# GpSimd issues its loads in program order instead of the scheduler's order, in a weight-gradient matmul with seven products for eight

## The chip, the cores and the metric

The kernel runs on one core of one Trainium2 chip. The metric is the device time of one execution in microseconds (us), as the median of several runs. The profile is one execution on the same core; its span, 166.3 us, is the part between the first and the last recorded instruction and is about 2 us shorter than the device time.

## The reference

```python
def setup_inputs():
    batch, m, k, n = 16, 512, 1024, 768
    return {
        "input": np.random.randn(batch, m, k).astype(np.float32),
        "grad_output": np.random.randn(batch, m, n).astype(np.float32),
    }

def reference(input: np.ndarray, grad_output: np.ndarray) -> np.ndarray:
    grad_weight = np.einsum('bmk,bmn->kn', input, grad_output)
    return grad_weight.astype(np.float32)
```

Batch and rows are one contraction of 16 x 512 = 8192 rows: the output, 1024 x 768, is the sum over all rows of x (1024 columns) times g (768 columns). Both inputs are float32 in the chip's main memory, 33.6 MB and 25.2 MB.

## The kernel before, in words

**Slices and loads.** The 8192 rows are 64 slices of 128 rows. `LOADS` has 32 letters, one for each load `u` of two slices. Eight loads `s` come first, then twenty `P`, then four `s`. An `s` gives two single items, one a slice. A `P` gives one item of two slices, which is computed with fewer products (below). For each load there is a tile `xp` (128 x 2 x 1024, bf16) and a tile `gp` (128 x 2 x 768, bf16). GpSimd issues the transfers that fill them, and these turn float32 into bf16 on the way. For the first eight loads (`u < MERGED`) each slice has its own transfer: `gp` on line 111 (192 KB written), `xp` on line 113 (256 KB). From load 8 on there is one transfer of both slices: `gp` on line 106 (384 KB), `xp` on line 107 (512 KB). In the program `gp` stands ahead of `xp` each time. The very first data (`xf` for slices 0 and 1, `gf` for slice 0) come as float32 through the queues of SyncE and ScalarE and are rounded by VectorE and ScalarE on line 203.

**Buffers.** `gp` and `xp` of load 0 have a pool of their own. All later ones, with `xf` and `gf`, share a pool of `PAIRS_HELD = 14` buffers for each of the two kinds, so a load may be issued when an earlier tile in its buffer is done with. Each GpSimd transfer also signals on one of eight semaphores, taken in turn. A transfer waits until the one issued eight before it has landed. So at most eight are under way at once.

**Products.** For an `s` item the output is four quadrants, called A, B (upper rows), C, D (lower rows); A and C take the left columns of g, B and D the right ones. For a `P` item the two slices and the two halves of columns form a 2 x 2 by 2 x 2 block product, done with seven products instead of eight: A and D, and five others `n p m o q`. They need sums and differences of halves: `ge` from `gp` (lines 131, 135), `gp` changed in place (line 140), `xe` from `xp` (lines 145, 149), `xp` in place (line 154). VectorE makes these, all in bf16.

**TensorE.** `ORDER` is written out by hand. A step such as `A9` means: bring product A up to item 9, with the weights from x and the moving operand from g, 128 x 384 at a time into a bank (line 278), for four blocks q. `A9!0,0,0,0` also closes the product: its four banks are added to the float32 sums `acc` or `macc`, by ScalarE (line 292) or VectorE (line 296), and after block q the given number of VectorE's sums for coming pairs (`filler`) is placed there. At the end `macc` is shared out to `acc` (line 163 and others), and finished blocks go to memory through SyncE's queue. The first steps are:

```
"A1:4 C1:4!0,0,0,0 B2:4!0,0,0,0 A2 D1:2 A3!0,0,0,0 D2 D3 D4 C4:4!0,0,0,0 D5 B5:2 D6!0,0,0,0 "
"B6 A6:2 B7 B8 A7 A8 A9!0,0,0,0 ...
```

**What sets the order on each engine.** A planner orders the instructions of an engine by its own estimate of times, unless the engine is named in `manual_schedule`. Before the change TensorE, VectorE and ScalarE are named, so they run in the order of the program. GpSimd is not, so its transfers stand in the planner's order.

Of the kernel before, what the change touches and what calls it, by code (L numbers as in the profile page):

```python
# [42 lines left out]
def kernel(  # L43
# [30 lines left out]
    SLOT = {"n": 0, "p": 1, "m": 2, "o": 3, "q": 4}  # L74

    E = mybir.EngineType
    ctx.enter_context(tc.manual_schedule(engines={E.PE, E.DVE, E.Activation}))

    xf = [pairs.tile([P, K], f32, name=f"xf{s}", tag="xp") for s in range(2)]
    gf = pairs.tile([P, N], f32, name="gf", tag="gp")  # L80
# [308 lines left out]
```

## Time and profile before

| | |
|---|---|
| device time, median of 3 runs | 168.19 us (168.03 to 168.38) |
| span of the profile | 166.3 us |
| TensorE (PE) busy | 159.8 us, 96% of the span |
| VectorE (DVE) busy | 118.6 us, 71% |
| ScalarE (ACT) busy | 87.6 us, 53% |
| GpSimd (POOL) busy | 41.1 us, 25% |
| granted TensorE clock | 1.00 |
| moved by DMA, as the page counts it | 33.39 MB, of it 28.64 MB through GpSimd's queue |

The page lists groups of instructions as: line, engine, operation, output tile and input tile, shape, count; then busy time, mean of one, and the idle time of the engine just ahead of them with what ended it. A timeline row is: start, duration, engine, line, operation, tiles, count, and in brackets the idle time before it and its releaser. GpSimd's rows in it (`DMA_DIRECT2D`) are [...]0.53 us each, not the transfer itself. A transfer's landing is the last of sixteen increments of its semaphore[...].

### The profile page before, as it was taken

Reading aid. Unit: us, or ns where it says so; the run is one execution under the profiler, and the core shown is the slowest. Engines: PE = TensorE matmul, PEld = TensorE weight load, DVE = VectorE, ACT = ScalarE, POOL = GpSimd, SP = SyncE. Lnnn points to the kernel's source line nnn. Section 1 sums busy time; section 2 is a strip of 40 time slices with the busy share of each in tenths; the row PEclk is TensorE's granted clock in tenths of the full one; section 3 lists DMA queues with packets and bytes.
Section 4 is the critical chain, followed back from the end, with each engine's and each line's share of the span. In section 5 each row is a group of like instructions: output and inputs, shape, how many; then the busy total and the mean of one; then the engine's idle time right before and its main releaser. Section 6 shows DMA issues by size and latency. Waiting matters only on the chain.

```text
span 166.3 us, 2688 instructions
## 1 busy us (share of the span) xinstructions
PE 159.8 (96%) x963; PEld 93.5 (56%) x963; DVE 118.6 (71%) x240; ACT 87.6 (53%) x206; POOL 41.1 (25%) x81
## 2 busy tenths in 40 slices
PE   8799999999999999999999999899999999999992
PEld 2356656565655655665565655455656656565661
DVE  0400221121979879878979998989999899999992
ACT  3779413330486768755648476756677878100000
POOL 7444444544122222222212222222221000000000
PEclk9999999999999999999999999999999999999999
DMA  5999999999999999999999999999999999105555
GB/s 181 287 209 208 211 206 208 208 209 217 211 216 211 215 212 214 210 215 210 215 211 214 211 213 212 217 211 212 212 217 213 214 210 209 25 0 189 189 189 189
DMA packets 14124, 33.39 MB, mean 201 GB/s; under 512 B 1568, under 2 KB 5920, under 8 KB 14112
## 3 DMA queue, kind: packets, MB, share of 16 engines
q0 software_dynamic: 11088, 28.64, 88.5%
q1 hardware_dynamic: 2736, 3.54, 6.0%
q10 hardware_dynamic: 288, 1.05, 1.7%
q8 instruction: 7, 0.11, 0.3%
q14 instruction: 5, 0.04, 0.1%
HBM read 58.72 MB, written 3.15 MB: 372 GB/s over the span
## 4 chain that ended last, share of the span: by engine, by line
PE 76%; DVE 16%; DMA 5%; POOL 1%; issue 1%; DVEq 0%; POOLq 0%
PE bank L278 75%; DVE macc L296 5%; DMA xp<-in_input_dram 5%; DVE gp L140 2%; DVE xe L145 2%; DVE acc L296 2%; DVE ge L131 2%; DVE xp L154 1%; POOL gp L111 1%; DVE ge L135 1%; DVE xe L149 1%; PE bank L328 0%; DVE acc L336 0%; DVEq L296 0%; POOLq L373 0%
## 5 line engine op out<-in xcount | busy, mean ns | idle before, releaser
L278 PEld LDWEIGHTS <-xp 128*128 128x128 bf16 x697 | 67.6, 98 | 49.4 <-issue 1.9
L278 PE MATMUL bank<-gp,xp 128*128 128x384 bf16 x537 | 92.4, 326 | 2.0 <-DVE xp L203 0.8
L292 ACT COPY acc<-bank 128x384 f32<-128x384 f32 x55 | 24.4, 487 | 31.2 <-PE bank L278 31.1
L296 DVE TENSOR_TENSOR acc<-bank,acc 128x384 f32<-128x384 f32 x46 | 23.7, 552 | 21.3 <-PE bank L278 21.0
L292 ACT COPY macc<-bank 128x384 f32<-128x384 f32 x61 | 27.3, 492 | 20.2 <-PE bank L278 20.1
L278 PEld LDWEIGHTS <-xe 128*128 128x128 bf16 x240 | 23.2, 98 | 16.6 <-DVE xe L145 1.4
L278 PE MATMUL bank<-ge,xp 128*128 128x384 bf16 x160 | 29.8, 326 | 0.2
L278 PE MATMUL bank<-gp,xe 128*128 128x384 bf16 x160 | 28.3, 326 | 0.3 <-DVE xe L145 0.2
L296 DVE TENSOR_TENSOR macc<-bank,macc 128x384 f32<-128x384 f32 x37 | 19.4, 553 | 5.3 <-PE bank L278 5.0
L107 POOL DMA_DIRECT2D xp<-in_input_dram x24 | 12.7, 530 | 36.9 <-DMA xp<-in_input_dram 20.3
L106 POOL DMA_DIRECT2D gp<-in_grad_output_dram x24 | 12.7, 530 | 32.7 <-PE bank L278 19.5
L268 ACT COPY bank<-macc 128x384 f32<-128x384 f32 x43 | 19.3, 490 | 0.0
L268 ACT COPY bank<-acc 128x384 f32<-128x384 f32 x41 | 18.4, 501 | 0.0
L163 DVE TENSOR_TENSOR acc<-acc,macc 128x768 f32<-128x768 f32 x16 | 14.5, 950 | 0.0
L145 DVE TENSOR_TENSOR xe<-xp 128x1024 bf16<-128x1024 bf16 x20 | 13.7, 684 | 0.7 <-DMA xp<-in_input_dram 0.7
L278 PE MATMUL bank<-ge,xe 128*128 128x384 bf16 x80 | 14.1, 326 | 0.0
L154 DVE TENSOR_TENSOR xp<-xp 128x1024 bf16<-128x1024 bf16 x20 | 13.7, 683 | 0.0
L131 DVE TENSOR_TENSOR ge<-gp 128x768 bf16<-128x768 bf16 x20 | 11.0, 550 | 0.1
L140 DVE TENSOR_TENSOR gp<-gp 128x768 bf16<-128x768 bf16 x20 | 11.0, 551 | 0.0
L113 POOL DMA_DIRECT2D xp<-in_input_dram x14 | 7.5, 538 | 9.0 <-DMA xp<-in_input_dram 6.4
L111 POOL DMA_DIRECT2D gp<-in_grad_output_dram x15 | 8.2, 547 | 6.1 <-DMA gp<-in_grad_output_dram 4.6
L294 DVE COPY acc<-bank 128x384 f32<-128x384 f32 x2 | 1.0, 554 | 10.6 <-PE bank L278 10.6
(19 smaller groups left out, 34.3 us busy)
## 6 DMA issues: line engine op xcount, KB each, us to landing
xp<-in_input_dram POOLq DMA_DIRECT2D x24, 512.0 KB, 16.9
gp<-in_grad_output_dram POOLq DMA_DIRECT2D x24, 384.0 KB, 16.7
xp<-in_input_dram POOLq DMA_DIRECT2D x14, 256.0 KB, 8.5
gp<-in_grad_output_dram POOLq DMA_DIRECT2D x15, 192.0 KB, 8.5
out_dram<-acc SPq DMA_DIRECT2D x15, 192.0 KB, 1.9
xf<-in_input_dram ACTq DMA_DIRECT2D x2, 512.0 KB, 5.0
gf<-in_grad_output_dram SPq DMA_DIRECT2D x2, 192.0 KB, 4.3
out_dram<-acc SPq DMA_DIRECT2D x1, 128.0 KB, 1.7
```

The lines of the kernel that those rows point to most:

```text
L106: nc.gpsimd.dma_start(out=gp, in_=G[rows, :].rearrange("(p m) n -> p m n", m=2))
L107: nc.gpsimd.dma_start(out=xp, in_=X[rows, :].rearrange("(p m) k -> p m k", m=2))
L111: nc.gpsimd.dma_start(out=gp[:, h, :], in_=G[s * P : (s + 1) * P, :])
L131: nc.vector.tensor_add(out=ge[:, 0:2, :], in0=g[:, :, 0, :], in1=g[:, :, 1, :])
L140: nc.vector.tensor_sub(out=g[:, 1:3, :], in0=g[:, 1:3, :], in1=g[:, 3::-3, :])
L145: nc.vector.tensor_add(out=xe[:, 0:2, :].rearrange("p a k -> p (a k)"), in0=xp[:, 0, :], in1=xp[:, 1, :])
L154: nc.vector.tensor_sub(out=x[:, 1:3, :], in0=x[:, 1:3, :], in1=x[:, 0::3, :])
L163: nc.vector.tensor_add(out=dst, in0=dst, in1=macc[:, slots, q, :])
L268: nc.scalar.copy(out=bank, in_=sum_of(p, q))
L278: nc.tensor.matmul(bank, stat, mov, start=opening and j == 0 and not carried, stop=close and j == len(items_now) - 1, skip_group_check=car ...
L292: nc.scalar.copy(out=dst, in_=bank)
L296: nc.vector.tensor_add(out=dst, in0=bank, in1=dst)
```

## The change

```diff
     E = mybir.EngineType
-    ctx.enter_context(tc.manual_schedule(engines={E.PE, E.DVE, E.Activation}))
+    ctx.enter_context(tc.manual_schedule(engines={E.PE, E.DVE, E.Activation, E.Pool}))
```

GpSimd (`Pool`) is named as well, so its 77 transfers are issued as the program has them: `gp` and then `xp` of each load, load by load. The aim is that data are asked for in the order in which the program uses them. The number and the sizes of the transfers, the instructions of all other engines, and the buffers' addresses remain. In two places the order of issue is a different one. Loads are numbered from 0; h0 and h1 are the two slices of a load:

```
place 1   before: gp0 h1, gp1 h0, gp1 h1, xp1 h0, xp1 h1, gp2 h0, ...
          after:  gp0 h1, gp1 h0, xp1 h0, gp1 h1, xp1 h1, gp2 h0, ...

place 2   before: ... gp23 xp23 xp24 xp25 gp24 gp25 gp26 gp27 xp26 gp28 xp27 xp28 gp29 xp29 xp30 gp30 gp31 xp31
          after:  ... gp23 xp23 gp24 xp24 gp25 xp25 gp26 xp26 gp27 xp27 gp28 xp28 gp29 xp29 gp30 xp30 gp31 xp31
```

## The prediction

> **What bounds the kernel now.** I read the head of the page first, then the chain that ended last, then the waits of TensorE's two rows, of VectorE and of GpSimd, and then the timeline of the places that the change touches.
>
> ```profile
> PE 159.8 (96%) x963; PEld 93.5 (56%) x963; DVE 118.6 (71%) x240; ACT 87.6 (53%) x206; POOL 41.1 (25%) x81
> DMA  5999999999999999999999999999999999105555
> PE 76%; DVE 16%; DMA 5%; POOL 1%; issue 1%; DVEq 0%; POOLq 0%
> ```
>
> PE is all but full, and the DMA engines are full until about 142 us. The chain is PE for three quarters; its DVE part lies between 63 and 124 us, where PE stops eight times, mostly for DVE, 2.6 us in all by the starts of its matmuls. That stretch has the same instructions after the change. What the change can touch is waiting for loads. The waits of PE's weight loads and of DVE (total us, times, longest), then the chain's first pieces:
>
> ```profile
> PEld L278 <- DMA xp<-in_input_dram: 0.8, 2, 0.6
> DVE xe L145 <- DMA xp<-in_input_dram: 0.7, 1, 0.7
> ```
>
> ```profile
> 1.23 1.70 POOL gp L111 x3
> 2.93 7.67 DMA xp<-in_input_dram
> 10.65 52.52 PE bank L278 x322
> ```
>
> In the whole run PE's weight loads waited twice for a load, and DVE's sums once. The chain says that the first of these, the landing of xp1 h0, set the start of 52 us of unbroken PE work. The timelines of PEld and PE show both:
>
> ```profile
> 10.64 12.79 PEld L278 LDWEIGHTS <-xp 128*128 128x128 bf16 x80 [0.59 <-DMA xp<-in_input_dram]
> 23.64 1.42 PEld L278 LDWEIGHTS <-xp 128*128 128x128 bf16 x10 [0.20 <-DMA xp<-in_input_dram]
> ```
>
> ```profile
> 7.61 2.83 PE L278 MATMUL bank<-gp,xp 128*128 128x384 bf16 x15 [0.56 <-DVE xp L203]
> 10.65 35.92 PE L278 MATMUL bank<-gp,xp 128*128 128x384 bf16 x220 [0.20 <-DMA xp<-in_input_dram]
> ```
>
> The second wait cost PE nothing: its weight load came late, but the matmul behind it started at 23.659, one normal step of 0.1625 us after the one ahead (23.496). It has no slack either. This is xp4 h0, which step `A9` needs. The timeline of GpSimd shows why it cannot come sooner:
>
> ```profile
> 2.93 1.08 POOL L113 DMA_DIRECT2D xp<-in_input_dram  x2
> 12.18 0.53 POOL L113 DMA_DIRECT2D xp<-in_input_dram  x1 [0.77 <-DMA xp<-in_input_dram]
> 14.35 0.53 POOL L113 DMA_DIRECT2D xp<-in_input_dram  x1 [0.73 <-DMA xp<-in_input_dram]
> 23.88 0.53 POOL L113 DMA_DIRECT2D xp<-in_input_dram  x1 [0.49 <-DMA xp<-in_input_dram]
> ```
>
> Each issue starts about 0.28 us after the landing of the transfer issued eight before it. xp4 h0 is issued at 14.35 and lands, by its last semaphore event, at 23.59; the issue eight later starts at 23.88. So eight transfers are always queued and the pace is that of the data.
>
> [...] So an order of issue moves places in one line and makes no bandwidth; the trace agrees, with landings every 0.91 to 0.95 us for 192 KB and 1.2 to 1.3 us for 256 KB. [...] The trace shows seven packets of 16 KB on the instruction queue, about 20 us apart at first (the work of 128 matmuls takes 20.8 us), the first at 20.456 us, lasting 0.945 us. It falls on a single DMA engine: of gp4 h0's sixteen increments fifteen came by 21.62, the last at 22.58, and xp4 h0's fifteenth came at 22.88, its last at 23.59. That is what makes xp4 h0 the tight one.
>
> **The change part by part.** The instructions of PE, DVE and ACT and the buffers' addresses are the same in both programs. No transfer is added or removed, so GpSimd's 77 issues cost what they did. What moves:
>
> Place 1. The third and fourth transfers in line swap. Before, by the landing events: gp1 h0 8.40, gp1 h1 9.35, xp1 h0 10.60, xp1 h1 11.90. After: xp1 h0 at 8.40 + 1.25 = 9.65, gp1 h1 at 10.60, and xp1 h1 at 11.90 as before. The matmul ahead of the wait started at 10.121, so the next can start at 10.121 + 0.1625 = 10.284 instead of 10.648: PE gains **0.36 us** here. gp1 h1 is needed at 12.61 - 0.36 = 12.25 and is there at 10.60.
>
> Then the gain meets the next loads. The need of each before less 0.36, against its landing: xp1 h1 12.09 against 11.90; xp2 h0 14.69 against 14.06; xp2 h1 17.29 against 16.31; xp3 h0 20.54 against 18.47; xp3 h1 21.19 against 20.72; xp4 h0 23.28 against **23.59**. The last fails. Its landing is unchanged, since the same bytes and the same instruction fetch lie ahead of it on the slowest engine. PE stops there and starts again where it did: weights at 23.635, matmul at about 23.64 against 23.659. Left of 0.36 us: about **0.01 to 0.02 us**.
>
> One second-order effect: PE ahead by 0.36 asks for its fetch at about 20.09 instead of 20.456. On the slow engine this is inside xp3 h1 and no longer behind it, and could delay xp3 h1 by up to 0.945, to 21.66. Its weights would then load at about 21.70, its matmul start at about 21.71, against 21.71 before. So the gain would go at xp3 h1 already; the result is the same.
>
> One wait is other: the issue of xp3 h0 waits for the third transfer, now at 9.65 instead of 9.35. It starts about 0.3 us later, at 9.93, and behind it GpSimd's next issue waits for 10.60 as before. Seven transfers are queued meanwhile, some 7.5 us of data; hidden.
>
> Place 2. xp24 and xp25 go behind their gp, xp26 and xp27 likewise. From xp23 (108.41), with 1.85 us for a gp and 2.45 for an xp as in the landings before, after: gp24 110.3, xp24 112.7, gp25 114.6, xp25 117.0, gp26 118.9, xp26 121.3, gp27 123.2, xp27 125.6, gp28 127.5, xp28 130.0, gp30 136.1, xp30 138.6. First uses before: gp24 115.59, xp24 117.62, gp25 119.62, xp25 121.75, gp26 124.22, xp26 126.59, gp27 128.13, xp27 129.57, gp28 and xp28 138.2; loads 29 to 31 from 142.9 on. The shortest slack is 3.9 us, where before gp24 had 0.38. But DVE did not wait for gp24 either: its rows are closed.
>
> ```profile
> 115.13 0.55 DVE L296 TENSOR_TENSOR macc<-bank,macc 128x384 f32<-128x384 f32 x1
> 115.59 0.55 DVE L131 TENSOR_TENSOR ge<-gp 128x768 bf16<-128x768 bf16 x1
> ```
>
> So place 2 gains nothing and costs nothing. Its waits for free buffers are on work done 20 us or more earlier (by the release times in the trace of before), and the last landing stays at about 142.9. Sum: -0.02 us, for a time of 168.19 - 0.02 = **168.17 us**.
>
> **Rivals.** (a) The head start is kept, because xp4 h0 lands sooner in the new order or in most runs. For it: PE's work is unbroken from 10.65 to 63.2, so what is gained there goes on. Against it: xp4 h0 had no slack, and the line ahead of it holds the same bytes. It gives 168.19 - 0.36 = 167.83; half of it kept, 168.0. (b) Slower: the later issue of xp3 h0 (0.3 us), or the earlier fetch, delays xp4 h0 or xp3 h1 beyond the need. For it: xp4 h0 passes each delay to PE one for one, and the fetch of 0.945 us is known to decide here. Against it: seven transfers are queued. It gives 168.19 + 0.30 = 168.49. (c) Place 2 helps, if DVE in ordinary runs is often held by gp24; the profile has slack of 0.38 there and DVE's list of waits has no such row, so at most a few tenths: about 167.9.
>
> **How the numbers follow.** Forecast (gain lost at xp4 h0, place 2 hidden) 0.72; (a) 0.12; (c) 0.05; (b) 0.11. So faster 0.17, same 0.72, slower 0.11. 0.2% is 0.34 us. The range takes in the full gain and the full loss and about 0.1 us of scatter, since three runs before lay within 0.17 us of their median: 167.73 to 168.58.
>
> **What would show it.** Right: PE's first long block starts at about 10.28, PE stops 0.2 to 0.4 us at a weight load at about 21.7 or 23.6 with an xp transfer as releaser, and from 23.7 to 124 us the rows are those of before. GpSimd's last issue stays near 125.6. Wrong: no stop there and DVE's first wait at 63.27 moved to about 62.9 (rival a), or that wait moved to 63.5 or later (rival b), or DVE rows between 115 and 130 us that move against PE's (c).

## The result, and the profile after

| | before | after |
|---|---|---|
| device time, median of 6 runs | 168.22 us (168.03 to 168.65) | 168.12 us (167.85 to 168.46) |
| ratio after/before, 95% interval | | 0.9995 (0.9978 to 1.0012) |
| span of the profile | 166.3 us | 166.7 us |

The change makes no difference that these runs can tell. A second set of 13 runs of the changed kernel (run e5 below) gave 1.0002 (0.9994 to 1.0010).

The head of the page is nearly what it was, but the DMA share is gone from the chain that ended last:

```profile
PE 160.6 (96%) x963; PEld 94.1 (56%) x963; DVE 118.5 (71%) x240; ACT 87.6 (53%) x206; POOL 41.0 (25%) x81
...
PE 80%; DVE 16%; ACT 1%; issue 1%; DVEq 0%
```

The chain in order of time (start, us, what) shows what took its place:

```profile
0.78 4.64 PE bank L89 x12
5.42 1.53 PE bank L278 x5
6.95 0.02 issue
6.97 1.63 ACT acc L292 x4
8.60 0.61 ACT xp L203 x2
9.21 0.05 issue
9.26 54.30 PE bank L278 x333
```

In this execution TensorE did not wait for xp1 h0 at all. It was late for another reason: the twelve warm-up matmuls and the first real ones ran at half speed for longer. The warm-up matmuls of 512 columns start 0.43 us apart up to 5.00 us in the profile after; in the one before they do so up to 4.14 us, and then 0.26 and 0.22 us apart. The first real matmuls start 0.32 us apart in the profile after and 0.16 us apart in the one before. The busy time of each engine in the stretch from 4.2 to 6.7 us (in brackets how many instructions started there; TensorE comes first), before and then after, has 13 matmuls against 10. The granted clock, third from the end, reads 1.00 in both and does not show it:

```profile
4.20:6.70 2.50, 2.17 (x13) 1.12 (x12) 1.20 (x5) 1.55 (x5) 1.40 (x3) 1.00 1.08 336
```

```profile
4.20:6.70 2.50, 2.50 (x10) 1.16 (x9) 1.14 (x5) 1.04 (x3) 1.39 (x3) 1.00 1.08 337
```

The trace's clock events have full speed from 4.22 us on before and from 6.72 us on after. The moment varies from run to run, and what sets it is not shown: in the thirteen of the fourteen profiles of this study that recorded it (all but e10), it lies between 3.50 and 6.75 us, and kernels with the same start have it early (e4, 3.94 us) and late (the profile after, 6.72 us). In the profile after, ScalarE's first bank copies (line 292) start at 6.97 us, where they started at 6.20 before; the rounding of slice 1 stands behind them (line 203, to 9.21 us), and xp1 h0 is long there (9.79 us) when TensorE comes to it at 10.89. In the old order it would have landed at about 10.74 (an estimate: the landing of gp1 h1, which has taken its place in the line), still in time. In such an execution place 1 has nothing to give.

Place 2 is as predicted. gp24 lands at 110.36 us and is used at 115.98; in VectorE's timeline the row (line 131) follows the one ahead of it without a gap, as before:

```profile
115.51 0.55 DVE L296 TENSOR_TENSOR macc<-bank,macc 128x384 f32<-128x384 f32 x1
115.98 0.55 DVE L131 TENSOR_TENSOR ge<-gp 128x768 bf16<-128x768 bf16 x1
```

### The profile page after: what moved, and what is told of

The parts are those of the page before. It is cut to its first block, busy times and chain, and to the rows that moved or that the text cites. A ratio compares the mean times of both kernels' runs of the same rounds, so it can differ in the third digit from the quotient of the medians.

```text
span 166.7 us, 2688 instructions
## 1 busy us (share of the span) xinstructions
PE 160.6 (96%) x963; PEld 94.1 (56%) x963; DVE 118.5 (71%) x240; ACT 87.6 (53%) x206; POOL 41.0 (25%) x81
## 4 chain that ended last, share of the span: by engine, by line
PE 80%; DVE 16%; ACT 1%; issue 1%; DVEq 0%
PE bank L278 77%; DVE macc L296 5%; PE bank L89 3%; DVE gp L140 2%; DVE xe L145 2%; DVE acc L296 2%; DVE ge L131 2%; DVE xp L154 1%; ACT acc L292 1%; DVE ge L135 1%; DVE xe L149 1%; PE bank L328 0%; DVE acc L336 0%; ACT xp L203 0%; DVEq L296 0%
## 5 line engine op out<-in xcount | busy, mean ns | idle before, releaser
L278 PE MATMUL bank<-gp,xe 128*128 128x384 bf16 x160 | 28.3, 326 | 0.3 <-DVE xe L145 0.2
```

Source lines behind the costliest of these rows:

```text
L278: nc.tensor.matmul(bank, stat, mov, start=opening and j == 0 and not carried, stop=close and j == len(items_now) - 1, skip_group_check=car ...
```

## The experiments

The theory: place 1 gives TensorE a head start, and a load that lands just in time takes it back; place 2 moves loads that are early in either order. Rivals: one place gains what the other loses; the head start is hardly ever there; what stands behind it is not a load. In the runs that move single loads the transfers are put in a list and issued in the order of the list, with some names moved behind others; all else is the changed kernel. The ratios are estimated from all runs of both kernels and differ by up to 0.0006 from the quotient of the medians. The kernel before, run beside them, has a median of 168.30 us for e1 to e4, 168.35 for e5 to e8 and 168.41 for e9 to e12.

**e1, place 1 alone, and e2, place 2 alone.**

```diff
 e1:
+    moved = {"x24": "x23", "x25": "x24", "x26": "g27", "x27": "g28", "g30": "x30"}   # late loads as before
 e2:
+    moved = {"x1.0": "g1.1"}                                                         # early loads as before
```

> Place 1 alone: xp1 h0 ahead of gp1 h1 as in the change, the late loads in the old order. Theory (the head start is lost at xp4 h0, which has no slack): within 0.1 us of before, 168.2. Theory that place 1 gains and place 2 gives it back: 0.36 us faster, 167.85. Theory that place 1 costs through a later issue: 0.3 us slower, 168.5. In a profile whose clock is granted early, PE's long block starts at about 10.28 and PE stops some 0.3 us at a weight load at 21.7 or 23.6; in one whose clock is granted late, neither is there.

> Place 2 alone: the early loads in the old order, the late ones gp, xp, gp, xp as in the change. Theory (the late loads are early enough in both orders): within 0.1 us of before, 168.2, and VectorE's rows from 108 to 130 us keep their distances. Theory that place 2 hides a loss or a gain of its own: 0.2 to 0.4 us off before, with VectorE or TensorE waiting for a load between 110 and 143 us.

Measured: e1 168.46 us, ratio 1.0011 (1.0005 to 1.0018) in 21 runs; e2 168.25 us, 0.9996 (0.9988 to 1.0004). So place 2 does nothing, and place 1 alone gains nothing and may cost a tenth of a per cent. TensorE's weight loads in e1:

```profile
9.01 12.63 PEld L278 LDWEIGHTS <-xp 128*128 128x128 bf16 x79 [0.80 <-ACT xp L203]
22.53 7.43 PEld L278 LDWEIGHTS <-xp 128*128 128x128 bf16 x47 [0.90 <-DMA xp<-in_input_dram]
```

The clock came late in this profile (6.23 us), and xp1 h0's weights were loaded at 10.65 us, no earlier than in the profile before. In the old order they would have had to wait until about 10.87 here (an estimate, again from the landing of gp1 h1), so some 0.2 us were gained. The wait at 22.53, which stops TensorE's matmuls for 0.68 us, takes more than that. It is for xp3 h1. Fifteen of its sixteen increments had come by 20.97, the last came at 22.49. TensorE's first instruction fetch (that it is TensorE's is inferred; the last section says from what), one packet of 16 KB, had started at 20.453 and took 0.949 us. The DMA queues from 20.3 to 21.5 us show it (queue, kind: packets, MB, share of the time of 16 engines):

```profile
q0 software_dynamic: 159, 0.24, 109.0%
q8 instruction: 1, 0.02, 4.9%
```

So in e1 the fetch fell into xp3 h1's packets, and one of that load's sixteen increments came 1.52 us after the other fifteen. Before, it started at 20.456 too, when xp3 h1 was not yet through either (15th increment 20.69, last 20.72), but did not hold it up. What differs is how much of the load was left. Take the time from the fetch's start to the moment when the load would have been there without it; where the load was held up, that moment is estimated as its 15th increment and the lag that xp3 h0 had behind its own. It is 0.71 us in e1 and 0.93 to 1.03 us in e4, e9 and e11, which were held up. It is 0.26 to 0.56 us in the profiles where the fetch started within xp3 h1 and did not hold it up (before, e2, e3, e6, e10).

**e3 and e4, the old and the program's order, with xp4 h0 needed later.** Product A is closed one item earlier, and C8 comes ahead of B9. By the order of the matmuls this also moves the first use of xp3 h1 four matmuls (0.65 us) later, and that of xp4 h1 and xp5 h0 four matmuls sooner:

```diff
-    "B6 A6:2 B7 B8 A7 A8 A9!0,0,0,0 B9 C9:2 C10!0,0,0,0 B11 ...
+    "B6 A6:2 B7 A7 A8!0,0,0,0 B8 C8:2 B9 C9 C10!0,0,0,0 B11 ...
```

> Old order of loads, and TensorE's hand order changed so that item 8 (xp4 h0) is needed 16 matmuls, 2.6 us, later: A closes after item 7 and C8 comes before B9. All is computed. Theory: alone it gains nothing, 168.2, because PE is not held up by xp4 h0 in the old order (0.00 to 0.02 us).

> Program order of loads as in the change, with the same later need of item 8. Theory (xp4 h0 takes the head start): with it out of the way the head start of 0.36 us goes through to VectorE's first wait and the end, up to 0.36 us below the old order with the same hand order, 167.85, in executions whose clock is granted early. Rival (the start itself is set by when the full clock is granted and by the rounding of slice 1, not by xp1 h0, in most executions): no difference to the old order in those, PE's long block starting at 9.2 to 9.3 without a wait for xp1 h0 in both, and a difference of the medians well under 0.36 us.

Measured: e3 168.21 us, 0.9992 (0.9986 to 0.9999); e4 168.22 us, 0.9990 (0.9981 to 0.9998). The two orders don't differ by more than the runs scatter. For e3 no gain was expected; its interval lies just below 1. Two other profiles of the old order show what the later need can save: TensorE stopped 0.18 us for xp4 h0 in e6 (landed at 24.00 us) and 0.06 us in e2, and in e3 it doesn't. The clock was granted early in both profiles (3.50 and 3.94 us), so they can be laid side by side. TensorE's weight loads, first in the old order:

```profile
8.84 1.24 PEld L278 LDWEIGHTS <-xp 128*128 128x128 bf16 x8
10.89 19.13 PEld L278 LDWEIGHTS <-xp 128*128 128x128 bf16 x119 [0.81 <-DMA xp<-in_input_dram]
```

and in the program's order:

```profile
8.82 3.19 PEld L278 LDWEIGHTS <-xp 128*128 128x128 bf16 x20
12.22 9.54 PEld L278 LDWEIGHTS <-xp 128*128 128x128 bf16 x60 [0.21 <-DMA xp<-in_input_dram]
22.30 5.80 PEld L278 LDWEIGHTS <-xp 128*128 128x128 bf16 x37 [0.54 <-DMA xp<-in_input_dram]
28.42 1.58 PEld L278 LDWEIGHTS <-xp 128*128 128x128 bf16 x11 [0.32 <-DMA xp<-in_input_dram]
```

The wait for xp1 h0 at 10.89 is gone: this is the head start (xp1 h0's weights at 10.12). At 22.30 there is the wait for xp3 h1 again, whose last increment came 1.26 us after the 15th, with a fetch at 20.21. TensorE stops 0.32 us there and 0.10 us at 28.4, for xp5 h0, which this hand order needs sooner. The matmul of xp1 h0 starts 0.61 us earlier than in e3, the last matmul 0.16 us (162.91 us against 163.07). So 0.16 us was kept in this pair of profiles, and nothing in the medians. xp4 h0, which the prediction had named first, was not needed to take the rest.

**e5, the changed kernel again.**

> The changed kernel itself once more, in more runs beside the kernel before, since place 1 alone came out 0.11% slower and place 2 alone 0.04% faster. Theory (place 1 moves TensorE's own instruction fetch onto the slow DMA engine while xp3 h1 is under way, which costs as often as the head start gains): like place 1 alone, 0 to 0.1% slower, 168.3 to 168.5. Rival (the change is a plain nothing and the 0.11% came by chance): within 0.05% of before.

Measured: 168.38 us beside 168.35 before, 1.0002 (0.9994 to 1.0010). The runs don't settle whether place 1 costs the 0.1% of e1: the intervals of e1 and e5, which have the same early loads, overlap between 1.0005 and 1.0010. The profile again had a late clock (6.75 us) and no wait for a load.

**e6 to e8, moving the instruction fetch.** In the ten profiles with twelve warm-up matmuls the first fetch starts at TensorE's 95th to 98th matmul, those of the warm-up counted, whenever that comes (19.90 to 20.82 us). So warm-up matmuls were added or taken away to move it:

```diff
 e6, old order of loads:
-WARMUP = [512] * 10 + [128] * 2
+WARMUP = [512] * 10 + [128] * 5
 e7, program order; e8, program order and the hand order of e3 and e4:
-WARMUP = [512] * 10 + [128] * 2
+WARMUP = [512] * 9
```

> Old order of loads; three more tiny warm-up matmuls (128 columns), which fit in TensorE's idle time before its first real matmul but put six more instructions ahead, so that the first instruction fetch comes about three matmuls, 0.49 us, sooner: at 19.9 to 20.1. Theory (a fetch inside xp3 h1's packets delays that load by up to the fetch's 0.95 us): xp3 h1 lands near 21.7 to 22.3 instead of 20.7, TensorE stops 0.1 to 0.8 us at its weight load, and the median is 0.2 to 0.6 us slower, 168.5 to 168.9. Rival (the fetch does not matter, only the bytes ahead do): no stop, 168.2 to 168.3.

> Program order of loads; warm-up of nine matmuls instead of twelve, so that the first instruction fetch comes about 0.49 us later, behind xp3 h1's packets again. Theory: xp3 h1 lands near 20.8, no stop there; where TensorE has its head start it stops at xp4 h0 (landing 23.6 to 23.9) instead; 168.1 to 168.2. Rival (fetch does not matter): as the changed kernel. If the shorter warm-up delays the full clock, the first block is later and the median is 168.4 or more.

> As the run before, and the hand order that needs item 8 2.6 us later. Theory (those two loads, xp3 h1 through the fetch and xp4 h0 through the bytes ahead of it, are all that took the head start): no stop of TensorE between its first long block and 65 us, and the head start reaches the end: 167.8 to 168.0. Rival (something further on, such as a VectorE sum that waits for a load near 48 to 61 us, takes it): no stop of TensorE before 65 us, but 168.2.

e6 missed its aim: the fetch came at 20.38 us, not at 20.0, with 0.56 us of xp3 h1 left (last increment 20.94). It did not hold the load up, and TensorE did not stop there. 168.37 us, 0.9996 (0.9986 to 1.0006). It says nothing of a fetch deep inside xp3 h1's packets.

e7 moved it further than meant, to 22.15 us: behind xp3 h1, which landed at 20.86, and into xp4 h0. That load's 15th increment came at 23.02 and its last at 24.19. The weight loads:

```profile
8.92 14.24 PEld L278 LDWEIGHTS <-xp 128*128 128x128 bf16 x88
24.23 5.80 PEld L278 LDWEIGHTS <-xp 128*128 128x128 bf16 x37 [1.08 <-DMA xp<-in_input_dram]
```

Measured 168.61 us, 1.0011 (1.0004 to 1.0019): the wait changed its load and TensorE's matmuls stopped 0.86 us for it. This is what the fetch theory says of a fetch there: the early loads stand in the order of e4 and e11, and xp3 h1 is held up no more once the fetch is elsewhere. The time that was expected (168.1 to 168.2) was too low. The shorter warm-up alone does not explain it, as e8 and e12 have it too and are not slower.

e8: 168.22 us, 0.9986 (0.9978 to 0.9994), above the 167.8 to 168.0 expected. With xp3 h1 clear of the fetch and xp4 h0 needed later, TensorE ran from 8.5 to 49.6 us without a stop of its matmuls over 0.1 us. Then VectorE's timeline has

```profile
47.93 0.69 DVE L145 TENSOR_TENSOR xe<-xp 128x1024 bf16<-128x1024 bf16 x1 [0.91 <-DMA xp<-in_input_dram]
```

and TensorE's weight loads

```profile
49.61 0.44 PEld L278 LDWEIGHTS <-xp 128*128 128x128 bf16 x4 [0.46 <-DVE xp L154]
```

The load is xp9, landed at 47.91 us (47.95 before). VectorE waited 0.66 us for it before and now 0.91 us, and TensorE waits for VectorE's sum. The rival named in the expectation holds for the load and the place, a third load that lands just in time; it had not expected TensorE to stop, which it does for 0.24 us.

**e9, a transfer more ahead of gp4 h0; e10 and e11, two more ahead of gp24, in the old and in the program's order.** They fill a spare tile that nobody reads:

```diff
+    spare = head.tile([P, N], bf16, name="spare")
 e9, program order:
+    load("spare", spare, G[0:P, :])       # issued behind xp3 h1
 e10, old order; e11, program order:
+    load("spare1", spare, G[0:P, :])      # issued behind xp19
+    load("spare2", spare, G[0:P, :])      # issued behind xp23
```

> Changed kernel with one transfer more, 192 KB into a spare tile that nobody reads, behind xp3 h1 and so ahead of gp4 h0. Theory (up to some 60 us the stream of loads sets the pace, with xp4 h0, xp9 and xp12's neighbours landing within 0.1 us of their use): every later load lands 0.93 us later and nearly all of that reaches the end: 0.6 to 0.95 us slower, 169.0 to 169.3, TensorE stopping 0.6 to 0.9 us at xp4 h0. Rival (the loads have slack and the end is set by VectorE between 63 and 124 us): 168.4.

> Old order of loads, with two transfers more of 192 KB into a spare tile that nobody reads, one behind xp19 and one behind xp23: 1.87 us more of loading ahead of gp24. Theory (in the old order gp24 lands 0.38 us ahead of its use): VectorE waits about 1.5 us for gp24 at 115.6, and about 1.2 us of it reaches the end, 169.4 to 169.7. Rival (place 2 has slack in either order): 168.3 to 168.4.

> Program order of loads, with the same two transfers more. Theory (in the program's order the shortest slack of the late loads is 3.9 us): no wait of VectorE or TensorE for a load after 65 us, time as without them, 168.3 to 168.4. Rival (any delay of the stream reaches the end): as the old order, 169.4 or more.

e9: 169.45 us beside 168.41, 1.0060 (1.0048 to 1.0072), so 0.8 to 1.2 us for one transfer of about 0.93 us, a little above the 169.0 to 169.3 us expected. Within that interval the early stream of loads passes the delay on in full:

```profile
22.40 1.74 PEld L279 LDWEIGHTS <-xp 128*128 128x128 bf16 x12 [1.14 <-DMA xp<-in_input_dram]
24.93 5.15 PEld L279 LDWEIGHTS <-xp 128*128 128x128 bf16 x33 [0.80 <-DMA xp<-in_input_dram]
```

The first is xp3 h1 with the fetch inside, the second xp4 h0, which lands 1.3 us later than before. TensorE's matmuls stop 0.92 and 0.57 us. The first stop is not the extra transfer's doing, since that stands behind xp3 h1.

e10: 169.20 us, 1.0047 (1.0035 to 1.0059). e11: 168.42 us, 0.9998 (0.9989 to 1.0007). VectorE in the old order, then in the program's order:

```profile
115.11 0.55 DVE L298 TENSOR_TENSOR macc<-bank,macc 128x384 f32<-128x384 f32 x1
116.95 0.56 DVE L133 TENSOR_TENSOR ge<-gp 128x768 bf16<-128x768 bf16 x1 [1.29 <-DMA gp<-in_grad_output_dram]
```

```profile
115.44 0.55 DVE L298 TENSOR_TENSOR macc<-bank,macc 128x384 f32<-128x384 f32 x1
115.91 0.55 DVE L133 TENSOR_TENSOR ge<-gp 128x768 bf16<-128x768 bf16 x1
```

The same 1.87 us of loading costs 0.8 us in the old order and nothing in the new. That is what place 2 brings: slack, not time. The expected 1.2 us at the end was too much: VectorE's wait was 1.29 us, TensorE's stops behind it grew by 1.0 us in the profile, and the runs have 0.6 to 1.0 us.

**e12, the reliefs together.** As e8, and all of slice 1 rounded by VectorE:

```diff
-            round_by("ACT", x1, xf[1], 6 * P, 8 * P)
+            round_by("DVE", x1, xf[1], 6 * P, 8 * P)
...
-            round_by("ACT", x1, xf[1], 2 * P, 4 * P)
+            round_by("DVE", x1, xf[1], 2 * P, 4 * P)
```

> The kernel with program order, item 8 needed later and nine warm-up matmuls, and with the rounding of all of slice 1 on VectorE, so that it no longer stands behind ScalarE's bank copies where the clock comes late. Theory (TensorE's start can be made earlier, but xp9 at 47.9 us holds VectorE and then TensorE): TensorE's long block starts at 9.9 to 10.2, no stop before 48 us, VectorE waits about 1 us for xp9, and the end is that of the run with item 8 needed later, 168.1 to 168.25. Rival (the start is worth what it saves): 167.8 or less.

Measured: 168.21 us beside 168.41, 0.9987 (0.9980 to 0.9994). The end is as expected, but the start was not earlier (xp1 h0's weights at 10.19 us), and the first stop was not at 48 us: xp5 h0, landed at 28.27, stopped TensorE for 0.25 us at 28.3. At 47.2 it stopped 0.18 us for a reason that the profile does not name, and VectorE waited 0.69 us for xp9 at 47.95. e8 and e12 are the best kernels here, 0.13 to 0.14% below the kernel before. What part the order of loads has in that is not shown: e3, with the old order, has 0.9992, its interval overlaps theirs, and the old order was not run with the shorter warm-up.

## Why the prediction was right

**Right: no measurable change, by a head start that is lost to a later load.** The forecast was 168.17 us; measured 168.12. The experiments show the mechanism: xp1 h0's weights were loaded at 10.12 to 10.27 us in the six program-order profiles whose clock came by 5.15 us (e4, e7, e8, e9, e11, e12), and at 10.63 to 10.89 in the four with the old order that stopped there (before, e3, e6, e10). The predicted head start is there, and no profile brings it to the end in full. The plainest case is e11, which is the changed kernel up to xp19 and had an early clock (3.65 us). Its matmul of xp1 h0 started at 10.36 us, against 10.65 before, and then TensorE stopped 0.62 us for xp3 h1:

```profile
8.90 12.28 PEld L280 LDWEIGHTS <-xp 128*128 128x128 bf16 x76
22.02 7.91 PEld L280 LDWEIGHTS <-xp 128*128 128x128 bf16 x50 [0.84 <-DMA xp<-in_input_dram]
```

**Off: which load takes it, and how much.** The prediction put the stop at xp4 h0 and named xp3 h1 with the instruction fetch as a second-order effect, with a landing of at most 21.66 us and the same result. That TensorE's head start brings the fetch forward by as much, to 20.09 us, was its estimate; in e4 the fetch started at 20.21. In the program order with the old warm-up the first load that stopped TensorE was xp3 h1 each time there was a stop (e1, e4, e11, and e9 with its extra transfer), and it landed at 21.98 to 22.49. The delay was put at no more than the fetch's 0.945 us; the last increment came 1.15 to 1.52 us after the 15th instead. So the stop, 0.32 to 0.68 us without the extra transfer, could be longer than the head start. In the five profiles with the old order of early loads (before, e2, e3, e6, e10) the fetch never delayed xp3 h1: its last increment came 0.02 to 0.10 us after the 15th. What adds 0.2 to 0.6 us to the fetch's own time stays open. That xp4 h0 has no slack was right: it stopped TensorE in e2 and e6 with the old order and in e7, and was used 0.07 us after it landed in the profile after.

**Not foreseen: the start of TensorE varies more than the change is worth.** In the changed kernel's own two profiles (after, e5) neither sign that the prediction named was there: the long block started at 9.26 and 9.27 us without a wait for xp1 h0, and no matmul of it was held up by more than 0.1 us until 65 us. The full clock came at 6.6 us or later in them and in e2, and TensorE had nothing to gain from an earlier xp1 h0. So no change is what comes out in both kinds of execution, and the prediction had the reason for one; that the other gives the same number is luck. The forecast's start of the long block at 10.28 us was read from one execution with an early clock, as if that were the kernel's own. In four of the thirteen profiles with a clock on record it came at 6.2 us or later (those three and e1); how often it does in the other runs is not known. The scatter was also read a little low: the three runs before lie up to 0.19 us from their median, not 0.17, which changes nothing here.

**Place 2: right.** The order of issue made no bandwidth: the last of the 77 loads landed at 142.91 us before and at 143.01 after. The landings worked out came within 0.2 us of the profile after (gp24 110.36 against 110.3; xp27 125.76 against 125.6; the last load 143.01 against 142.9), e2 moved nothing, and e10 and e11 show where the slack is. In both profiles each issue started 0.28 to 0.62 us after the landing of the one issued eight before it (the prediction's 0.28 us is that of the early loads), so no wait for a free buffer shows. The later issue of xp3 h0 (10.07 us, with 9.93 worked out) was hidden: it landed at 18.61 and was needed at 21.29.

**The rivals.** (a), the head start kept: not shown in the runs of the changed kernel or of e4; 0.16 us of it in the pair of profiles of e3 and e4. That TensorE's work was unbroken up to 63.2 us did not mean that a gain goes on: VectorE used xp9 0.02 us after it landed already before, and e8, with both early stops out of the way, lost 0.24 us there. (b), slower through the fetch: e1 and e7 are 0.11% (0.19 us) slower, less than the 0.30 us named, and each one's only profile has the stop that a fetch makes; for the change itself it is not shown. (c), place 2 helps: no.

## What to carry to other kernels

A wait that is taken away pays only as far as the next thing that lands just in time, so list the slack of everything behind it before pricing it; here four loads in the 48 us behind xp1 h0 (xp4 h0, xp9, xp10 and gp12) were used less than 0.1 us after they landed, in the profile before. Where loads queue eight deep and the stream is full, as here, an order of issue gives slack to some (gp24 landed 0.38 us ahead of its use before and 5.6 us after) and takes it from others (xp25: 8.4 us before, 5.0 us after), and an extra load, added to the old and to the new order, tells in two runs which it was (1.87 us more of loading cost 0.8 us in e10 and nothing in e11). And look at the start of several executions before a few tenths of a microsecond near the start are believed: TensorE's long block started at 10.65 us in the profile before and at 9.26 us in the one after.

## What the runs showed of the hardware that was not expected

An instruction fetch is traffic among the loads: one packet of 16 KB. The fourteen in the profiles before and after took 0.89 to 1.21 us, ten of them 0.93 to 0.98. With a fetch under way, one of a load's sixteen increments came late and the other fifteen did not: of gp4 h0's, before, fifteen had come by 21.62 us and the last came at 22.58. That this is one DMA engine held up, the slow engine of the prediction, is inferred from the one increment; no view names the engine of a packet. The last increment of a load that TensorE itself waited for came more than a microsecond after the 15th in e1, e4, e9 and e11 (xp3 h1, 1.15 to 1.52 us) and in e7 (xp4 h0, 1.17 us). That the fetches are TensorE's is inferred too: each profile has seven, in the profile before 94 to 138 matmuls apart, the first comes at the 95th to 98th matmul in the profiles with twelve warm-up matmuls, and TensorE has by far the most instructions (1949 records in the profile before, no other engine has 300).

When the fetch starts is not a simple count of matmuls. With twelve warm-up matmuls the first one started at TensorE's 95th to 98th matmul; with fifteen at its 98th, with nine at its 105th or 106th. Why fewer warm-up matmuls moved it so far stays open.

The moment of the full clock spread over 3.25 us (3.50 to 6.75). With the early loads in program order, xp1 h0's weights were loaded at 10.12 to 10.27 us where it came by 5.15 us, and at 10.65 to 10.91 us where it came at 6.23 us or later (e1, after, e5). That is about as much as the times of one and the same kernel scatter (168.06 to 168.87 us for the kernel before, beside e5 to e8).
